# Output projections with the tokens in the partitions, and the seams between the layers in a fixed order

## The chip, the cores and the metric

The kernel runs on one core of a Trainium2 chip. The metric is device time in microseconds (us) of one execution. The core's engines are TensorE (PE, with its weight loads as PEld), VectorE (DVE), ScalarE (ACT), GpSimd (POOL) and SyncE (SP), which issues all the transfers here.

## The reference

The model is three layers over 512 tokens of width 1024: gated linear attention (GLA), native sparse attention (NSA) and a hybrid layer (stick-breaking attention, a causal pool, two branches). What the change touches are the joints between them:

```python
for i in range(2):                                   # i = 0: GLA, i = 1: NSA
    h = rms_norm(x, pre_norm[i])
    y = gla_mixer(h, ...) if i == 0 else nsa_mixer(h, ...)   # each ends in  o @ w_out
    x = x + rms_norm(y, post_norm[i])
# the hybrid layer
h = rms_norm(x, norm_gain) * (1 + scale) + shift     # shift, scale, gate from c
...
merged = sigmoid(m_a) * p_a + sigmoid(m_b) * p_b
x = x + gate * (merged @ w_out)
return rms_norm(x, final_gain)
```

## The kernel before, in words

Activations lie feature-major: `x` is [128 features, 8 chunks, 512 tokens]. Every product in near full precision is three matmuls in fp32r: operands are split into a high part (cast on ACT) and the rest (subtraction on DVE), and high x high, high x low and low x high are summed in PSUM. The activations' parts are `hH` and `hL`; a weight unit is 256 columns wide, comes as two halves through two raw buffers (L147), and is split by `load_unit` (ACT L150, DVE L151) into one of two buffers. `ORDER` lists the units, `prefetch` loads one ahead, a `None` in it is stepped over by `go_on`. PSUM is cut into banks by tag: `pj` 2, `sc` 3, `tr` 2, `pv` 1.

The order of instructions on each engine is found by the compiler's list scheduler, except in the slot loop of the stick-breaking stage, which stands in a `manual_schedule` of PE, DVE, ACT and POOL: there the order of the text holds, and weight splits are put in it by steps (`step`, `run_splits`).

The joints are `boundary` (L326): the layer's output product `out` (L240 to L242) makes feature tiles of 128 x 256 tokens; a token's norm is a sum over partitions, so squares are added up (`Squares`, L279 to L283), reduced with a ones-matmul (L289), put through `rsqrt` (some 13 small DVE steps), and spread over the partitions again with a diagonal matmul (`spread`, L299 and L300). `post` scales, adds the old `x` and squares again; `pre` does the second norm. At the first joint `pre` only gives `rc` and `rT`, one over the row norm, which NSA's consumers multiply in later (token projections L747 to L750, the rope tables, L809, L989). Products, `post` and `pre` of the two token halves are interleaved. Behind the first joint come the token projections of NSA (`w_tok`, 280 columns, L249 to L251), then units 4 and 7 at 512 columns (L208 to L210), from which `compress` (first matmul L828) is fed.

Behind the second joint come v of the first two groups (`sb_vs`), then q and k of group 0, then the slot loop `SB_SLOTS`: each slot scores a pair of heads (L1119, then ACT, POOL and DVE up to the POOL product `SW`, L1140), while PE does listed projections in pieces (L217 to L219) and the products of the pair before (transposes L401, products L1169). The last projections, of u, stay in their two `pj` banks and are copied out by `pool_diff` (L1251). The last product (`w_o2`) is again feature-major, with the final norm behind it (L1339 to L1346).

## Time and profile before

| | us |
|---|---|
| median of 3 runs | 1273.79 (1273.69 to 1275.81) |
| the profiled execution | 1269.81 |
| its span on the chip | 1268.1 |
| PE busy in the span | 1200.2 |
| DVE, ACT, POOL busy | 832.8, 610.1, 312.2 |
| mean granted clock of TensorE | 0.978 of 2.4 GHz |

A row of the view in order of time gives start, length, engine, line, operation and tiles; what stands in brackets is the idle time of that engine before it and what ended it. Matmuls overlap, so the distance from one start to the next is the price, not the length. A granted clock of 1.00 is 2.4 GHz, 0.50 is 1.2 GHz.

### The profile page before, as it was taken

Reading aid. Unit: us, or ns where it says so; the run is one execution under the profiler, and the core shown is the slowest. Engines: PE = TensorE matmul, PEld = TensorE weight load, DVE = VectorE, ACT = ScalarE, POOL = GpSimd, SP = SyncE. Lnnn points to the kernel's source line nnn. Section 1 sums busy time; section 2 is a strip of 40 time slices with the busy share of each in tenths; the row PEclk is TensorE's granted clock in tenths of the full one; section 3 lists DMA queues with packets and bytes.
Section 4 is the critical chain, followed back from the end, with each engine's and each line's share of the span. In section 5 each row is a group of like instructions: output and inputs, shape, how many; then the busy total and the mean of one; then the engine's idle time right before and its main releaser. Section 6 shows DMA issues by size and latency. Waiting matters only on the chain.

```text
span 1268.1 us, 18606 instructions
## 1 busy us (share of the span) xinstructions
PE 1200.2 (95%) x6800; PEld 1014.3 (80%) x6800; DVE 832.8 (66%) x1608; ACT 610.1 (48%) x1274; POOL 312.2 (25%) x432
## 2 busy tenths in 40 slices
PE   6999999889999999999999989999989999999996
PEld 6788778877866777777988968889868888888896
DVE  7678787675569888877578576777765453233554
ACT  6552136533437667669556566575543232212330
POOL 2123122221002433334121264555523400000000
PEclk9999999979999999999999989999989999999998
DMA  6254624325241011110343111111222222333332
GB/s 203 68 179 154 231 93 143 105 93 185 109 125 50 26 51 35 50 34 34 117 134 117 51 50 67 68 67 57 77 83 86 97 79 88 99 100 100 100 117 83
DMA packets 46362, 120.65 MB, mean 95 GB/s; under 512 B 5296, under 2 KB 19760, under 8 KB 45760
## 3 DMA queue, kind: packets, MB, share of 16 engines
q1 hardware_dynamic: 46272, 119.48, 28.7%
q8 instruction: 53, 0.87, 0.3%
q14 instruction: 37, 0.30, 0.1%
HBM read 109.50 MB, written 6.29 MB: 91 GB/s over the span
## 4 chain that ended last, share of the span: by engine, by line
PE 70%; DVE 10%; issue 7%; ACT 6%; DMA 4%; POOL 2%; SPq 0%; DVEq 0%; POOLq 0%; ACTq 0%
PE ps_pj L208 10%; PE ps_pj L209 10%; PE ps_pj L210 10%; PE ps_tr L401 3%; PE ps_pv L971 3%; PE ps_sc L209 2%; PE ps_sc L208 2%; PE ps_sc L210 2%; DVE w_lo L151 2%; PE ps_pj L217 2%; PE ps_pj L219 2%; PE ps_pj L218 2%; DMA wada<-in_w_ada_dram 2%; ACT w_hi L150 1%; PE ps_sc L828 1%
## 5 line engine op out<-in xcount | busy, mean ns | idle before, releaser
L208 PE MATMUL ps_pj<-hH,w_hi 128*128 128x512 f32 (+1 forms) x752 | 281.5, 375 | 9.4 <-DVE u L1251 5.9
L210 PE MATMUL ps_pj<-hH,w_lo 128*128 128x512 f32 (+1 forms) x752 | 280.8, 374 | 0.5 <-DVE w_lo L151 0.5
L209 PE MATMUL ps_pj<-hL,w_hi 128*128 128x512 f32 (+1 forms) x752 | 279.6, 372 | 0.0
L151 DVE TENSOR_TENSOR w_lo<-w_raw,w_hi 128x1024 fp32r<-128x1024 f32 (+1 forms) x154 | 190.4, 1248 | 101.0 <-ACT w_hi L150 101.0
L150 ACT CAST w_hi<-w_raw 128x1024 fp32r<-128x1024 f32 (+1 forms) x154 | 158.9, 1050 | 180.1 <-PE ps_pj L209 66.0
L208 PEld LDWEIGHTS ps_pj<-hH,w_hi 128*128 128x128 f32 x752 | 143.0, 190 | 35.1 <-DVE u L1251 6.0
L210 PEld LDWEIGHTS ps_pj<-hH,w_lo 128*128 128x128 f32 x752 | 143.3, 191 | 23.7 <-DVE w_lo L151 1.0
L209 PEld LDWEIGHTS ps_pj<-hL,w_hi 128*128 128x128 f32 x752 | 143.1, 190 | 23.3 <-issue 0.2
L959 POOL TENSOR_SCALAR PB<-PB,sm 128x128 f32<-128x128 f32 (+3 forms) x128 | 76.9, 621 | 183.6 <-DVE sm L955 183.6
L405 ACT CAST PTh<-ps_tr 128x512 fp32r<-128x512 f32 (+3 forms) x160 | 74.8, 480 | 65.8 <-PE ps_tr L401 61.8
L406 DVE TENSOR_TENSOR PTl<-ps_tr,PTh 128x512 fp32r<-128x512 f32 (+3 forms) x160 | 85.8, 550 | 27.0 <-ACT PTh L405 26.0
L952 ACT ACTIVATE PB<-ps_sc,nmx 128x128 f32<-128x128 f32 (+3 forms) x128 | 66.7, 533 | 16.8 <-PE ps_tr L401 5.5
L217 PE MATMUL ps_pj<-hH,w_hi 128*128 128x512 f32 x176 | 72.0, 409 | 0.0
L219 PE MATMUL ps_pj<-hH,w_lo 128*128 128x512 f32 x176 | 70.2, 399 | 0.0
L218 PE MATMUL ps_pj<-hL,w_hi 128*128 128x512 f32 x176 | 69.9, 397 | 0.0
L1136 DVE TENSOR_TENSOR_SCAN SF<-be,zero 128x128 f32<-128x128 f32 (+3 forms) x64 | 57.2, 915 | 11.6 <-POOL be L1129 11.3
L1140 POOL TENSOR_TENSOR SW<-sg,SF 128x512 f32<-128x512 f32 (+2 forms) x48 | 64.6, 1351 | 0.0
L401 PE MATMUL ps_tr<-ident,PB 128*128 128x128 f32 x320 | 50.9, 273 | 0.0
L249 PE MATMUL ps_pj<-w_hi,hH 128*128 128x256 f32 (+2 forms) x128 | 40.1, 316 | 9.8 <-ACT w_hi L485 8.3
L283 DVE TENSOR_TENSOR acc<-acc,sq 128x256 f32<-128x256 f32 x68 | 31.6, 465 | 24.4 <-ACT sq L282 17.5
L971 PE MATMUL ps_pv<-PTh,vv 128*128 128x512 f32 (+3 forms) x128 | 44.6, 355 | 0.7
L949 DVE TENSOR_REDUCE nmx<-ps_sc 128x1 f32<-128x384 f32 (+1 forms) x64 | 38.9, 617 | 9.6 <-PE ps_sc L948 9.1
(337 smaller groups left out, 2832.5 us busy)
## 6 DMA issues: line engine op xcount, KB each, us to landing
w_raw<-in_w_in_dram SPq DMA_DIRECT2D x64, 512.0 KB, 3.3
wada<-in_w_ada_dram SPq DMA_DIRECT2D x24, 512.0 KB, 3.7
w_raw<-in_w_nsa_dram SPq DMA_DIRECT2D x24, 512.0 KB, 3.9
w_raw<-in_w_gla_dram SPq DMA_DIRECT2D x22, 512.0 KB, 4.3
w_raw<-in_w_gla_out_dram SPq DMA_DIRECT2D x8, 512.0 KB, 3.6
w_raw<-in_w_nsa_out_dram SPq DMA_DIRECT2D x8, 512.0 KB, 3.3
w_raw<-in_w_bb_dram SPq DMA_DIRECT2D x8, 512.0 KB, 3.3
w_raw<-in_w_ba_dram SPq DMA_DIRECT2D x8, 512.0 KB, 3.6
```

The costliest lines, as they stand in the source:

```text
L150: S.copy(hi[:, :, s], raw)
L151: V.tensor_sub(lo[:, :, s], raw, f32(hi[:, :, s]))
L208: TE.matmul(p[:m, :tn], wh[:, k, s], aH[:, k, ts], start=(k == 0), stop=False)
L209: TE.matmul(p[:m, :tn], wh[:, k, s], aL[:, k, ts], start=False, stop=False)
L210: TE.matmul(p[:m, :tn], wl[:, k, s], aH[:, k, ts], start=False, stop=(k == KC - 1))
L217: TE.matmul(p, wh[:, k, s], aH[:, k], start=(k == 0), stop=False)
L218: TE.matmul(p, wh[:, k, s], aL[:, k], start=False, stop=False)
L219: TE.matmul(p, wl[:, k, s], aH[:, k], start=False, stop=(k == KC - 1))
L401: TE.transpose(pt[:, o:o + P], ws[e][:, OFF[qb] + kb * P:OFF[qb] + (kb + 1) * P], ident)
L406: V.tensor_sub(pl[:, :m], pt[:, :m], f32(ph[:, :m]))
L959: G.tensor_scalar(pbs[b][:, o], pbs[b][:, o], sm[:, qb, b:b + 1], 0.0, op0=ALU.mult, op1=ALU.add)
L971: TE.matmul(pv[:, kb * P:], vv[:, kb, b, g].rearrange("p e d -> p (e d)"), p_, start=first, stop=last and p_ is pair[1])
```

## The change

- The three output products (`w_gla_out`, `w_nsa_out`, `w_o2`) have the tokens in the partitions: eight blocks of 128 tokens x 512 features, two units of 256 columns each (`out_products`). The residual `x` is kept and reloaded token-major (`xR`, `x1d`, `x2d`, `xt`). A row's norm is then a sum along the free axis: `square_sum` on ACT with its accumulator, `rms` on DVE, gains as rows spread by a transfer (`row_of`). At the two joints the normed rows are transposed back on PE, eight transposes for a block of tokens, scaled on ACT, and split into `hH` and `hL`. `rc` and `rT` are gone from NSA.
- Each joint stands in a `manual_schedule` (`in_order`) from its first split to behind the first projections of the next layer; the second one goes on through the slot loop. Norm steps are generators in `chains`, moved on by `tick`; `need` moves them on where a projection wants their columns.
- Units 4 and 7 are projected by token halves, before the token projections of the second half; the rope of unit 4 stands in front of those.
- In `SB_SLOTS` the projection k(1, 0) moves from slot 1 to slot 0. u is copied out of PSUM in the slot loop.

```diff
@@ SB_SLOTS
-    ((0, 0), (("q", 1, 0), ("q", 1, 1))),
-    ((0, 1), (("k", 1, 0), ("k", 1, 1), ("za", 0, 0))),
+    ((0, 0), (("q", 1, 0), ("q", 1, 1), ("k", 1, 0))),
+    ((0, 1), (("k", 1, 1), ("za", 0, 0))),
@@ load_unit
+                splits.append((step + (late or lag) + j, hi, split))
+    def tick():
+        nonlocal step
+        step += 1
+        for ch in chains[:]:
+            while ch[0] <= step:
+                d = next(ch[1], None)
+                if d is None:
+                    chains.remove(ch)
+                    break
+                ch[0] = step + d
+        run_splits()
+    @contextmanager
+    def in_order():
+        nonlocal splits
+        E = mybir.EngineType
+        with tc.manual_schedule(engines={E.PE, E.DVE, E.Activation, E.Pool}):
+            splits = []
+            yield
+            while chains:
+                tick()
+            while splits:
+                splits.pop(0)[2]()
+        splits = None
@@ proj_toks (feats_pieces ticks every second k)
         for k in range(KC):
+            if need:
+                if k % max(1, 4 // len(jobs)) == 0:
+                    tick()
+                    ensure(*(u for u, _, _, _ in jobs))
+                need(jobs[0][1] * P, k)
...
+    def rms(ss):
+        v = npl.tile([P, 1], F32, tag="rsv1", name="rsv", bufs=2)
+        V.scalar_tensor_tensor(v, ss[:, 0:1], EPS, ss[:, 1:2], op0=ALU.add, op1=ALU.add)
+        return rsqrt(v, 1)
+    def square_sum(src, ss, n):
+        scr = npl.tile([P, 512], F32, tag="scr", name="scr", bufs=1)
+        S.activation(scr, src, AF.Square, scale=1.0 / 32, accum_out=ss[:, n:n + 1])
+    def out_products(us, each, freed=lambda: None):
+        for c in range(KC):
+            split_h(c, slice(0, 256), x[:, c, 0:256])
+        def second():
+            for c in range(KC):
+                split_h(c, slice(256, 512), x[:, c, 256:512])
+                yield c % 2
+        chains.append([step + 1, second()])
+        for b, n in ((0, 0), (1, 0), (2, 0), (0, 1), (1, 1), (3, 0), (2, 1), (3, 1)):
+            p = psum("sc" if b % 2 else "pj")
+            for i in range(2):
+                proj_toks([(us[2 * n + i], b, p[:, 256 * i:256 * i + 256], 256)], hH, hL, lambda t0, k: None)
+            each(b, n, p)
+            if (b, n) == (3, 0):
+                freed()
+    def boundary(wsrc, gain, xsrc, keep, scale, shift, then):
+        norms_, chunks = {}, [0] * NB
+        def norm(b, ss, xo):
+            y = rms(ss)
+            ss2 = npl.tile([P, 2], F32, tag="ss2", name="ss2", bufs=2)
+            for n in range(2):
+                xn_ = xt[:, b, half(n)]
+                V.scalar_tensor_tensor(xn_, xn_, y, grow[:, half(n)], op0=ALU.mult, op1=ALU.mult)
+                V.tensor_add(xn_, xn_, xo[n])
+                square_sum(xn_, ss2, n)
+            nc.sync.dma_start(keep[:, b], xt[:, b])
+            yield 4
+            y = rms(ss2)
+            xs = [npl.tile([P, 512], F32, tag="xs", name="xs", bufs=2) for n in range(2)]
+            for n in range(2):
+                S.activation(xs[n], xt[:, b, half(n)], AF.Copy, scale=y)
+            yield 4
+            ts = slice(b * P, b * P + P)
+            for n in range(2):
+                pt = psum("tr")
+                for i in range(4):
+                    TE.transpose(pt[:, i * P:(i + 1) * P], xs[n][:, i * P:(i + 1) * P], ident)
...
+                S.copy(hH[:, cs, ts], tmp)
+                V.tensor_sub(hL[:, cs, ts], tmp, f32(hH[:, cs, ts]))
+                chunks[b] += 4
+                yield 1
...
+        def each(b, n, p):
+            if n == 0:
+                SS[b] = npl.tile([P, 2], F32, tag="ss", name="ss", bufs=4)
+            S.copy(xt[:, b, half(n)], p)
+            square_sum(p, SS[b], n)
+            if n:
+                norms_[b] = [step + 2, norm(b, SS[b], [reload(xsrc, b, n_) for n_ in range(2)])]
+                chains.append(norms_[b])
+                if b == 2:
+                    nus.append(unit(*then[0]))
+        with tc.tile_pool(name="wout", bufs=2) as pool:
+            us = [unit(wsrc, u) for u in range(2)]
+            us += [load_unit(wsrc, u, pool=pool, late=4 * u - 3) for u in (2, 3)]
+            grow = row_of(gain)
+            out_products(us, each, go_on)
+            nus.append(unit(*then[1]))
@@ behind the first joint
+            ucs = [load_unit(w_nsa, u, pool=fp, late=5 + 4 * i) for i, u in enumerate((4, 7))]
...
+            toks((0, 1), ("pj", "pj", "sc", "sc"))
+            cks(0)
+            cks(256)
+        r1, r2 = rope(*PCK[0])
+        toks((2, 3), ("tr", "tr", "sc", "pv"))
@@ before the second joint
+    gated = dp.tile([KC, P], F32, name="gated")
+    nc.sync.dma_start(gated.rearrange("c p -> p c"), mod[:, 16:24])
@@ sb_proj
-                UP.append(p)
+                UP.append(u_first.tile([P, T], F32, name="u%d" % j))
+                V.tensor_copy(UP[j], p)
@@ the last product
+        x2 = pool.tile([P, NB, D], F32, name="x2", bufs=1)
+        nc.sync.dma_start(x2, x2d)
+        gate, fgain = row_of(gated.rearrange("c p -> (c p)")), row_of(fgain_r, "fgain")
+        def last(b):
+            y = rms(SS[b])
+            for n in range(2):
+                xn_ = xt[:, b, half(n)]
+                V.scalar_tensor_tensor(xn_, xn_, y, fgain[:, half(n)], op0=ALU.mult, op1=ALU.mult)
+                nc.sync.dma_start(out[:, b, half(n)], xn_)
+            yield 0
+        def each(b, n, p):
...
+            V.tensor_mul(xn_, p, gate[:, half(n)])
+            V.tensor_add(xn_, xn_, x2[:, b, half(n)])
+            square_sum(xn_, SS[b], n)
+            if n:
+                chains.append([step + 1, last(b)])
+        out_products(us, each)
```

## Rows read from the trace of the kernel before

**Rows 1.** The page, busy time, share of the span and instructions of each engine.
```profile
PE 1200.2 (95%) x6800; PEld 1014.3 (80%) x6800; DVE 832.8 (66%) x1608; ACT 610.1 (48%) x1274; POOL 312.2 (25%) x432
```
**Rows 2.** Waits of PE, whole run: us in total, times, longest.
```profile
PE ps_tr L289 <- DVE acc L283: 9.8, 4, 2.8
...
PE ps_tr L300 <- DVE rsd L299: 7.8, 5, 3.5
PE ps_pj L208 <- DVE u L1251: 5.9, 1, 5.9
PE ps_tr L401 <- POOL SW L1140: 5.0, 1, 5.0
```
**Rows 3.** PE in order of time: prices of 256 and 280 columns and of transposes.
```profile
238.46 0.28 PE L240 MATMUL ps_pj<-hH,w_hi 128*128 128x256 f32 x1
...
244.22 0.28 PE L240 MATMUL ps_sc<-hH,w_hi 128*128 128x256 f32 x1
...
263.74 0.28 PE L249 MATMUL ps_sc<-w_hi,hH 128*128 128x280 f32 x1
...
266.44 0.29 PE L249 MATMUL ps_sc<-w_hi,hH 128*128 128x280 f32 x1
...
603.54 1.06 PE L401 MATMUL ps_tr<-ident,PB 128*128 128x128 f32 x8
```
**Rows 4.** PE at the first seam's ends; then windows (PE, PEld, DVE, ACT, POOL, clock, DMA).
```profile
199.47 0.36 PE L240 MATMUL ps_pj<-hH,w_hi 128*128 128x256 f32 x1
...
317.68 2.58 PE L828 MATMUL ps_sc<-csp,cw 128*128 128x124 f32 x21 [1.31 <-issue]
...
275.00:280.00 5.00, 1.49 (x8) 1.37 (x7) 4.59 (x22) 1.56 (x5) 2.46 (x4) 0.50 0.65 214
```
**Rows 5.** DVE in order of time: subtractions of weights at two entries.
```profile
205.93 2.45 DVE L151 TENSOR_TENSOR w_lo<-w_raw,w_hi 128x1024 fp32r<-128x1024 f32 x2
...
1210.71 1.22 DVE L151 TENSOR_TENSOR w_lo<-w_raw,w_hi 128x1024 fp32r<-128x1024 f32 x1
```
**Rows 6.** PE in order of time, second seam: first product, last chunk, slot loop.
```profile
608.26 0.28 PE L240 MATMUL ps_pj<-hH,w_hi 128*128 128x256 f32 x1
...
618.20 0.51 PE L240 MATMUL ps_pj<-hH,w_hi 128*128 128x256 f32 x2 [0.50 <-ACT hH L304]
...
718.32 0.45 PE L217 MATMUL ps_pj<-hH,w_hi 128*128 128x512 f32 x1
```
**Rows 7.** POOL in order of time, first slot; then a window behind it.
```profile
735.14 3.03 POOL L1140 TENSOR_TENSOR SW<-sg,SF 128x512 f32<-128x512 f32 x2
...
740.00:760.00 20.00, 20.00 (x98) 16.72 (x96) 15.00 (x21) 12.77 (x24) 12.72 (x16) 0.95 0.16 53
```
**Rows 8.** Windows: the stretch behind the wait for u.
```profile
940.00:960.00 20.00, 20.00 (x81) 15.99 (x80) 14.65 (x27) 6.36 (x10) 7.49 (x10) 0.91 0.20 70
```
**Rows 9.** All engines in order of time: the last product and the tail.
```profile
1207.37 0.28 PE L208 MATMUL ps_pj<-hH,w_hi 128*128 128x256 f32 x1
...
1255.21 0.48 DVE L1339 SCALAR_TENSOR_TENSOR x<-ps_pj,mod,xr 128x256 f32<-128x256 f32 x1 [1.42 <-PE ps_pj L210]
...
1257.42 0.16 DVE L291 TENSOR_SCALAR rsv<-ps_tr 128x2 f32<-128x2 f32 x1 [0.76 <-PE ps_tr L289]
...
1259.59 0.16 DVE L266 SCALAR_TENSOR_TENSOR rsy<-rst,rsy 128x2 f32<-128x2 f32 x1
...
1261.45 3.22 DVE L1344 SCALAR_TENSOR_TENSOR x<-x,vec,ps_tr 128x256 f32<-128x256 f32 x8 [1.18 <-PE ps_tr L300]
```
**Rows 10.** Groups by line and shape: count, busy us, mean ns, idle before.
```profile
L405 ACT CAST PTh<-ps_tr 128x512 fp32r<-128x512 f32 x64 | 37.3, 586 | 24.0 <-PE ps_tr L401 23.4
...
L406 DVE TENSOR_TENSOR PTl<-ps_tr,PTh 128x512 fp32r<-128x512 f32 x64 | 43.2, 681 | 12.9 <-ACT PTh L405 12.7
```
**Rows 11.** DMA issues by line: count, KB each, median us to landing.
```profile
w_raw<-in_w_nsa_out_dram SPq DMA_DIRECT2D x8, 512.0 KB, 3.3
...
pe<-in_pe_k_dram SPq DMA_DIRECT2D x1, 8.0 KB, 8.3
```

More of the change, by code (lines that the diff above doesn't have):

```diff
@@ L155, in load_unit, with run_splits, ensure @@
             else:
-                splits.append((step + 2 + j, split))
+                splits.append((step + (late or lag) + j, hi, split))
         return hi, lo
-    def run_splits(all_=False):
-        while splits and (all_ or splits[0][0] <= step):
-            splits.pop(0)[1]()
-            if not all_:
-                return
+    def run_splits():
+        if splits and splits[0][0] <= step:
+            splits.pop(0)[2]()
+    def ensure(*units):
+        while splits and any(s_[1] is u_[0] for s_ in splits for u_ in units):
+            splits.pop(0)[2]()
+    def tick():
[19 more added lines that the diff above has]
+            while splits:
+                splits.pop(0)[2]()
+        splits = None
     ORDER = [(w_gla, u) for u in (8, 0, 2, 5, 6, 1, 3, 9, 10)]
-    ORDER += [(w_gla_out, 0), (w_gla_out, 1), None, (w_tok, 0), (w_tok, 1)]
-    ORDER += [(w_nsa, u) for u in (4, 7, 5, 6)]
+    ORDER += [(w_gla_out, 0), (w_gla_out, 1), None, (w_tok, 0), (w_tok, 1), None]
+    ORDER += [(w_nsa, u) for u in (5, 6)]
     ORDER += [(w_nsa, st_[1] + (8 if st_[0] == "z" else 0)) for st_ in NSA_STEPS if st_[0] in ("q", "z")]
@@ L299, in spread @@
             V.tensor_scalar(d, ident, y[:, b:b + 1], None, op0=ALU.mult)
-            TE.matmul(r[:, b * P:(b + 1) * P], ones, d, start=True, stop=True)
+            ds.append(d)
+        return ds
+    def spread(ds):
+        r = psum("tr")
+        for b in range(2):
+            TE.matmul(r[:, b * P:(b + 1) * P], ones, ds[b], start=True, stop=True)
         return r[:, :256]
@@ new lines, in row_scales, with half @@
+        S.copy(rT[:, t0:t0 + 256], spread(diagonals(y)))
+    xt = x.rearrange("p c t -> p (c t)").rearrange("p (b d) -> p b d", b=NB)
+    def half(n):
+        return slice(n * 512, n * 512 + 512)
+    def rms(ss):
[5 more added lines that the diff above has]
+        S.activation(scr, src, AF.Square, scale=1.0 / 32, accum_out=ss[:, n:n + 1])
@@ L706, in tile_kernel @@
         dump("gla_og", gz[:])
-    x1d = dp.tile([P, KC, T], F32, name="x1d")
-    rest = boundary(w_gla_out, "post0", xT, "pre1", keep=x1d)
+    x1d = dp.tile([P, NB, D], F32, name="x1d")
+    norms.close()
+    open_norms()
+    lag = 5
+    prefetch(2)
+    first = ExitStack()
+    first.enter_context(in_order())
+    o = VEC["pre1"][0]
+    uts, need = boundary(w_gla_out, post_r0, xR, x1d, vec[:, o:o + 8], None, ((w_tok, 0), (w_tok, 1)))
     dump("x1", x[:])
@@ L1201, in tile_kernel @@
         pvs = sb_pv()
-        E = mybir.EngineType
-        splits = []
-        with tc.manual_schedule(engines={E.PE, E.DVE, E.Activation, E.Pool}):
-            for n, (pair, prs) in enumerate(SB_SLOTS):
-                scores = sb_w(*pair) if pair else iter(())
-                projs = (None for pr_ in prs for _ in sb_proj(*pr_))
-                if n == 1:
-                    next(pvs)
-                for i in range(8):
-                    step += 1
-                    run_splits()
-                    if n and (n, i) != (1, 0):
-                        next(pvs, None)
-                    next(scores, None)
-                    for _ in range(4 * len(prs) * (i + 1) // 8 - 4 * len(prs) * i // 8):
-                        next(projs)
-                    if n:
-                        next(pvs, None)
-                for _ in projs:
-                    pass
-            for _ in pvs:
-                pass
-            run_splits(True)
-        splits = None
+        lag = 2
+        for n, (pair, prs) in enumerate(SB_SLOTS):
+            scores = sb_w(*pair) if pair else iter(())
+            projs = (None for pr_ in prs for _ in sb_proj(*pr_))
+            if n == 1:
+                next(pvs)
+            for i in range(8):
+                tick()
+                if n and (n, i) != (1, 0):
+                    next(pvs, None)
+                next(scores, None)
+                for _ in range(4 * len(prs) * (i + 1) // 8 - 4 * len(prs) * i // 8):
+                    next(projs)
+                if n:
+                    next(pvs, None)
+            for _ in projs:
+                pass
+        for _ in pvs:
+            pass
+        first.close()
         dump("sb_og", x[:])
@@ L1246, in pool_diff @@
             for j in range(2):
[L1247 to L1248 removed]
+                if ready:
+                    u0 = ready[j]
+                else:
+                    p = psum("pj")
                     proj_feat(uu, j, p, hH, hL)
[L1250 to L1251 removed]
+                    u0 = gp.tile([P, T], F32, tag="zt", name="u0", bufs=4)
+                    V.tensor_copy(u0, p)
                 cur = u0
```

276 lines of the change are left out of this document (120 added, 156 removed).

## The prediction, made before the changed kernel had run

> **What bounds the kernel now.** I read the page first: PE is busy in 95% of the span, no other engine in more than 66% [rows 1]. So PE's own work sets the time, and a change that leaves PE's columns alone can only win PE's idle time and the time it runs at half clock. The view of waits, for PE alone over the whole run, says who PE waits for [rows 2]: the sum of squares (9.8 us) and the spread of the row norm (7.8), both in the seams; the copy of u behind the stick-breaking stage (5.9, once); the product SW at the start of that stage (5.0, once). PE's idle time is 1268.1 - 1200.2 = 67.9 us in all; the four kinds above are 28.5 of it. Last I read PE in order of time in the seams, as the diff rewrites those. The sum is made against the profiled execution (1269.8 us, span 1268.1); the median of the runs shown is 4.0 higher, so the saving is taken off 1273.8 at the end.
>
> **Prices of PE's work at full clock**, as start-to-start times [rows 3]: 48 matmuls of 256 columns from 238.46 to 244.22, 0.120 each; 21 of 280 columns from 263.74 to 266.44, 0.129 each; eight transposes in 1.06, of which the last is some 0.27 long, so 0.11 each or less.
>
> **First seam (GLA output product to the compressed units).** Before, it runs from PE's first product at 199.47 to the first matmul of the compression at 317.68, 118.2 us [rows 4]. After, PE must do in the same stretch: 384 products of 256 columns, 46.1; 192 token projections of 280 columns, 24.7; units 4 and 7 in halves, 2 units x 2 x 2 halves x 24 = 192 of 256, 23.0 (96 of 512 columns before); and, new, 4 blocks x 8 transposes back, 32 x 0.11 = 3.5. The last 8 transposes of the GLA gate also lie in it, 0.8. Sum 98.1. What goes: the ones-matmuls over the squares, the spreads and the waits for them (one of the worst stretches, 275 to 280, has PE busy 1.49 of 5 us at clock 0.50 [rows 4]). What comes:
> - The entry. The auto order filled it with products of four tiles; now PE takes block (0,0) alone, and its second half needs both halves of unit 1's low part. DVE finished those at about 207.1 (first of the two at 205.93, 1.2 each) [rows 5]; PE would be there at about 203.3 to 204.2. I take 3.0, bounds 1.0 (if DVE takes that subtraction ahead of the second-half splits) and 3.8.
> - The row norm. By ticks of 12 matmuls (1.44 us) a block's transposes are emitted 8 ticks, 11.5 us, behind its norm. The chain needs: ten small DVE steps, 2.2 (a like row of them runs from 1257.42 to 1259.59 [rows 9]); four 512-wide DVE steps, 2.7 (0.68 each [rows 10]); the last square on ACT with its accumulator, about 0.8 (0.59 for a 512-wide ACT step [rows 10], and the read-out); 2.2 again; two scalings 1.2. That is 9.1 of 11.5. Blocks 0 and 1 are ready before the token projection asks, blocks 2 and 3 while it and the compressed units run. Cost 0, bounds 0 and 2 a block.
> - The rope of unit 4, its eight copies and the four adds now hide behind 96 token matmuls, 12.4 us; before, they hid behind unit 7's second product and the compression still waited 1.31 [rows 4]. 0.5, bounds 0 and 3.
>
> 98.1 + 3.0 + 0.5 = 101.6, so 16.6 us less; bounds 11 and 19.
>
> **Second seam (NSA output to the first scores).** Before: products from 608.26, the last NSA tile ready at 618.20, the first pieces of the slot loop at 718.32 [rows 6]. By 618.20 PE had already run 55 of 384 products. After, in order, it can run only 21 before chunk 7 is wanted. Left then: 363 x 0.120 = 43.6; tokens for v, 192 x 0.120 = 23.0; q and k by halves, 23.0; 32 transposes, 3.5. Sum 93.1, against 100.1 from 618.20: 7.0 less. Against it: PE idles some 4 us at the entry and starts again at half clock, about 1.0 (as behind the 5.0 us wait below); and the v, q, k tiles of the second half come out two at a time and in order, each bank waiting for an ACT and a DVE step, about 1.3. In its favour: ACT no longer has a weight cast in front of chunk 7's split, about 0.7. Gain 5.4; bounds 0 and 8.
>
> **The slot loop's start.** PE waits 5.0 for the POOL product SW, the two last of which run from 735.14 [rows 7], then runs at a mean granted clock of 0.95 over 20 us (a part at 1.2 GHz, the rest at 2.4), another 1.0. One more projection is moved into slot 0: 24 matmuls of 512 columns, not over 48 x 0.120 = 5.8 us of PE, which covers the wait. Slot 1 loses the same work, so part of the wait may come back there, and ACT and DVE have one more k tile in slot 0. Gain 4.5 of 6.0; bounds 0 and 6.
>
> **u.** The wait of 5.9 [rows 2] and 20 us at 0.91 behind it, 1.8 [rows 8], exist because two banks hold u until the stage's memory is freed. The copies (two of 0.68) now stand in the loop, and no wait for the next unit's splits is listed there. Gain 7.5; bounds 5.9 and 7.7.
>
> **Last product and tail.** Before, PE ends at 1255.2 and the span 12.9 later: one step and square, sum, ones-matmul, the rsqrt chain, spread, eight scalings, stores [rows 9]. After: 384 x 0.120 = 46.1 from 1207.4 [rows 9], plus the entry: unit 1's low part ends at 1211.9 (1210.71 + 1.22 [rows 5]), wanted at 1210.4, so 1.6. PE ends at 1255.1. Then multiply and add 1.4, square and accumulator 0.8, crossings 0.3, rsqrt 2.2, two scalings 1.3, stores 3.4 (last scaling before to the end: 1261.45 + 3.22 to 1268.1): 9.4. Gain 3.6; bounds 1 and 6. The reload of 2 MB of x2 in one transfer waits for the branch stage's memory; 0.5 MB takes 3.3 to land [rows 11], so 2 MB takes up to 13, and the first add wants it after 6. DVE then waits, PE does not, as four tiles lie between: 0, and 3 if the split of unit 3 slips behind it.
>
> **What costs nothing.** The rT multiplications of the z units (eight, DVE) go, but PE has no gap to win there. The write of gated has 1024 pieces of 4 bytes. The nearest row is an 8 KB load of 128 rows of 64 bytes, 8.3 us to landing [rows 11], queued with others. Its source is ready since the GLA stage and nothing reads gated until the end, so I take 0; the upper end is a rival below. The Trainium skill (DMA: Bandwidth & Descriptors, Rules for kernel authors) speaks against this write: a strided last dimension becomes one descriptor for each element. No row here shows such a write.
>
> **The sum.** 16.6 + 5.4 + 4.5 + 7.5 + 3.6 = 37.6. 1269.8 - 37.6 = 1232.2 for a profiled execution; 1273.8 - 37.6 = **1236** by the median. With all bounds at once the gain is 18 to 47; I give the forecast's own range as 1227 to 1250.
>
> **Rivals.**
> - *The ticks are too short.* ACT and DVE now take splits, evictions and norm steps in one fixed list. The chain leaves 2.4 of 11.5 us a block; a weight split in between takes DVE 1.22 a half [rows 5] and nearly as much on ACT, twice a unit, and six units fall in each seam. If two splits and an eviction fall in each block's chain, PE stands at the transposes for about 3 us, 8 blocks: 24 us. 1260. For it: PE can't pass its transposes. Against: most blocks have slack before their columns are wanted.
> - *Slower: casts that wait for their landing.* In ACT's list a cast stands at a set tick; if its transfer is late, evictions, squares, DVE's steps and PE's transposes all queue behind it. Its issue waits for one of two raw buffers, freed by the split before, and landing takes 3.3 [rows 11]. It decides once a cast waits longer than the 5.8 us that one spare tile of product gives PE. Then each of six units stops PE for 3.3 and 1.0 of half clock, 26 us a seam, 52 in both: 1288. Against: the code leaves 5 ticks (7.2 us) between issue and cast.
> - *The write of gated holds the queues* in front of the second seam. If each of its 1024 pieces takes what a row of the 8 KB load takes, it lasts 8 x 8.3 = 66 us [rows 11]; issued as the seam begins, it lets unit 2, wanted after 17 us, land some 45 late: 1281. Against: it can go out long before.
> - *It doesn't do what it says*: the seams end no sooner because the order is fixed only on four engines and SP's list stays automatic; only u and the slot remain or are lost again: 1262 to 1274.
>
> **How the numbers follow.** Forecast 0.70 (1227 to 1250); better than that 0.03; ticks too short 0.14 (1250 to 1270); no effect 0.05, half of it within 0.2%; casts that wait 0.06; gated 0.02. The range 1226 to 1256 takes in the forecast and the near half of the first rival, about 0.8. A measurement of this kernel tells about 0.2% (2.5 us) from no change: faster 0.89, same 0.03, slower 0.08.
>
> **What would show it.** Right: no PE wait on squares or spreads; the first seam about 102 us from the first product to the compression; the second about 95 from the last NSA chunk; no wait for SW over 2 us; the projection behind u following at once; 9 to 10 us from PE's end to the span's. Wrong: PE waiting at the new transposes for xs, or at a product for w_hi or w_lo in mid-seam; a new wait for SW in slot 1 or 2; a compression that waits for its added tokens; an end of PE's last product later than 48 us after its start.

## The result, and the profile of the changed kernel

The changed kernel takes 1290.05 us (median; 1288.54 to 1292.27), the kernel before, measured beside it, 1274.8. The ratio is 1.0117 (95% interval 1.0093 to 1.0141): 1.2% slower, where 3% faster was forecast. Its profiled execution has a span of 1290.3 us and PE's row of the page reads:

```profile
PE 1199.9 (93%) x6880; PEld 1018.1 (79%) x6880; DVE 808.9 (63%) x1534; ACT 626.7 (49%) x1308; POOL 279.9 (22%) x398
```

PE is busy for as long as before (1200.2, [rows 1]). All of the 22.2 us more is PE's idle time: 90.4 instead of 67.9. (The busy time holds what PE does at the lower clock, on which more below.) Cut at marks that both kernels have (first product of the GLA output projection, first score of the NSA stage, its last product, first piece of the slot loop, the loop's last product, first matmul of the last output projection), the span divides so:

| stretch, us of the profiled execution | before | after | forecast | measured |
|---|---|---|---|---|
| start to the GLA output projection | 199.5 | 202.3 | 0 | +2.8 |
| first seam: to the first NSA score | 177.0 | 188.2 | -16.6 | +11.2 |
| NSA stage: to its last product | 237.9 | 236.0 | 0 | -1.9 |
| second seam: to the slot loop | 103.9 | 124.8 | -5.4 | +20.9 |
| slot loop | 214.6 | 213.6 | -4.5 | -1.0 |
| from there to the last output projection | 274.5 | 268.7 | -7.5 | -5.8 |
| last output projection and tail | 60.7 | 56.8 | -3.6 | -3.9 |

(Before, 28 products of the second seam, 3.4 us, are done in the row above it, so 3.4 of the two measured numbers there cancel. One trace tells such a stretch to about 3 us: e4 below, whose seams are those of the kernel before, has 178.6 for the first seam and 106.7 for the second, against 177.0 and 103.9.) Three of the five terms came out with the right sign, the last two of them at about the right size. Both seams came out the other way, by 27.8 and 22.9 us if the 3.4 is taken off. The whole-run view of waits, for PE alone (line waited for, engine and line that ended the wait; total us, times, longest), has the squares of [rows 2] no more, has 0.5, 0.8 and 0.6 us left of the spreads, SW and u, and has this instead:

```profile
PE ps_pj L287 <- ACT w_hi L149: 16.5, 2, 8.5
PE ps_sc L287 <- ACT w_hi L149: 10.3, 3, 4.0
...
PE ps_pj L289 <- DVE hL L357: 4.3, 3, 2.4
...
PE ps_tr L442 <- ACT xs L436: 2.8, 2, 1.6
...
PE ps_pv L1285 <- DVE ov L1292: 2.2, 1, 2.2
...
PE ps_pj L236 <- DVE zt L1400: 1.3, 1, 1.3
```

PE waits for weight casts (L149), not for the row norm: only 2.8 us are spent at the new transposes (L442). The timeline of PE has the four long waits, one pair in each seam, always at the first product of a unit that follows the output projection: token units 0 and 1, then v units 8 and 9.

```profile
264.54 0.60 PE L287 MATMUL ps_pj<-w_hi,hH 128*128 128x280 f32 x1 [8.03 <-ACT w_hi L149]
...
278.11 0.60 PE L287 MATMUL ps_sc<-w_hi,hH 128*128 128x280 f32 x1 [3.78 <-ACT w_hi L149]
...
686.83 0.58 PE L287 MATMUL ps_pj<-w_hi,hH 128*128 128x256 f32 x1 [8.45 <-ACT w_hi L149]
...
700.51 0.42 PE L287 MATMUL ps_sc<-w_hi,hH 128*128 128x256 f32 x1 [4.01 <-ACT w_hi L149]
```

Why is the cast late? The timeline of SP, which issues the weights, shows the two halves of token unit 0 leaving at 222.84:

```profile
222.84 2.46 SPq L146 DMA_DIRECT2D w_raw<-in_w_tok_dram  x2
...
256.87 0.33 SPq L146 DMA_DIRECT2D w_raw<-in_w_tok_dram  x1
```

These loads take 4.2 us to land (median of the four, in the table of transfers), so they lay there by about 230. ACT's timeline in the stretch where PE stops (start, duration, line; in brackets the idle time before it and who ended it):

```profile
253.30 0.58 ACT L467 COPY x<-ps_pj 128x512 f32<-128x512 f32 x1
...
254.36 1.13 ACT L149 CAST w_hi<-w_raw 128x1120 fp32r<-128x1120 f32 x1
255.37 1.16 ACT L447 ACTIVATE ntmp<-ps_tr,vec 128x128 f32<-128x128 f32 x4
256.56 0.62 ACT L452 CAST hH<-ntmp 128x512 fp32r<-128x512 f32 x1
261.30 0.63 ACT L384 ACTIVATE scr<-x 128x512 f32<-128x512 f32 x1 [4.12 <-DVE x L429]
...
262.75 0.63 ACT L384 ACTIVATE scr<-x 128x512 f32<-128x512 f32 x1 [0.73 <-DVE x L429]
...
263.38 1.11 ACT L149 CAST w_hi<-w_raw 128x1120 fp32r<-128x1120 f32 x1
```

The second cast of token unit 0, for which PE stands from 256.51 to 264.54, is next in ACT's list behind the two squares of block 2's norm (L384). ACT does nothing for 4.12 us until DVE has the first half of block 2 ready, squares it, idles 0.73 for the other half, squares that, and only then casts a weight whose transfer had landed by about 230, some 33 us before. (L149 and L150 are the two halves of a weight split, L384 a sum of squares, L428 and L429 the scaling and adding of the first norm, L447 and L452 the eviction of the transposes.) DVE, in the same stretch:

```profile
257.21 0.69 DVE L453 TENSOR_TENSOR hL<-ntmp,hH 128x512 fp32r<-128x512 f32 x1 [0.37 <-ACT hH L452]
257.82 0.15 DVE L379 SCALAR_TENSOR_TENSOR rsv<-ss 128x1 f32<-128x1 f32 x1
...
259.59 0.16 DVE L307 SCALAR_TENSOR_TENSOR rsy<-rst,rsy 128x1 f32<-128x1 f32 x1
259.79 0.75 DVE L428 SCALAR_TENSOR_TENSOR x<-x,rsy,grow 128x512 f32<-128x512 f32 x1
...
261.97 0.69 DVE L429 TENSOR_TENSOR x<-x,xr 128x512 f32<-128x512 f32 x1
...
264.52 1.33 DVE L150 TENSOR_TENSOR w_lo<-w_raw,w_hi 128x1120 fp32r<-128x1120 f32 x1 [1.86 <-ACT w_hi L149]
```

DVE starts block 2's rsqrt at 257.82, late, because it first waited for ACT's hH; then ACT waits for DVE's scaling, and DVE in turn 1.86 for ACT's cast. Neither engine is full (49% and 63% of the run; 11.50 and 13.78 of 20 us in the row of 260 to 280 below). They wait for each other in two fixed lists, and PE waits for both. That ACT keeps to its list whatever is ready behind its head is what the Trainium skill (PSUM — Partial Sum Buffer, Engine vs sequencer instructions) states: ScalarE's and VectorE's queues are strictly first in, first out. This trace agrees, with the 4.12 us ahead of a ready cast.

Behind the waits PE runs slower. Two stretches of the first seam (length, PE busy, ..., granted clock, DMA share, GB/s):

```profile
260.00:280.00 20.00, 10.16 (x51) 9.31 (x52) 13.78 (x35) 11.50 (x24) 0.58 (x1) 0.68 0.34 121
280.00:300.00 20.00, 18.41 (x134) 17.98 (x133) 10.22 (x24) 11.57 (x27) 0.00 (x0) 0.89 0.44 130
```

From 265.90 to 274.33 stand 47 products of 280 columns, 0.179 each instead of the 0.129 of [rows 3]. The first seam up to its last token product took 124.7 us (202.27 to 326.93): 98.1 of work by the prediction's count, 18.5 idle, and 8.0 that are left for slower running. (The mean granted clock of this stretch is 0.92; of the 106.1 us that PE is busy in it, the missing 0.08 are 8.5.)

### The profile page after: what moved, and what is told of

It reads as the page before. It is cut to its first block, busy times and chain, and to the rows that moved or that the text cites. A ratio compares the mean times of both kernels' runs of the same rounds, so it can differ in the third digit from the quotient of the medians.

```text
span 1290.3 us, 18597 instructions
## 1 busy us (share of the span) xinstructions
PE 1199.9 (93%) x6880; PEld 1018.1 (79%) x6880; DVE 808.9 (63%) x1534; ACT 626.7 (49%) x1308; POOL 279.9 (22%) x398
## 4 chain that ended last, share of the span: by engine, by line
PE 57%; DVE 17%; ACT 11%; issue 7%; DMA 4%; POOL 4%; SPq 0%; DVEq 0%; ACTq 0%; POOLq 0%
PE ps_pj L236 6%; PE ps_pj L238 6%; PE ps_pj L237 5%; ACT w_hi L149 3%; DVE w_lo L150 3%; PE ps_tr L494 3%; PE ps_pv L1082 2%; PE ps_sc L238 2%; PE ps_sc L237 2%; PE ps_sc L236 2%; ACT PB L1063 2%; PE ps_pj L245 2%; POOL us L1375 2%; PE ps_pj L247 2%; PE ps_pj L246 2%
## 5 line engine op out<-in xcount | busy, mean ns | idle before, releaser
L150 DVE TENSOR_TENSOR w_lo<-w_raw,w_hi 128x1024 fp32r<-128x1024 f32 (+1 forms) x154 | 189.4, 1242 | 118.8 <-ACT w_hi L149 114.0
L149 ACT CAST w_hi<-w_raw 128x1024 fp32r<-128x1024 f32 (+1 forms) x154 | 159.2, 1050 | 151.3 <-PE ps_sc L237 62.4
L236 PE MATMUL ps_pj<-hH,w_hi 128*128 128x512 f32 x528 | 213.8, 405 | 7.8 <-DVE rtm L843 3.8
L237 PE MATMUL ps_pj<-hL,w_hi 128*128 128x512 f32 x528 | 211.9, 401 | 0.0
L238 PE MATMUL ps_pj<-hH,w_lo 128*128 128x512 f32 x528 | 211.8, 401 | 0.0
L238 PEld LDWEIGHTS ps_pj<-hH,w_lo 128*128 128x128 f32 x528 | 100.0, 189 | 20.9
L287 PE MATMUL ps_sc<-w_hi,hH 128*128 128x256 f32 (+1 forms) x312 | 92.5, 298 | 10.8 <-ACT w_hi L149 10.3
L289 PE MATMUL ps_pj<-w_hi,hL 128*128 128x256 f32 (+2 forms) x304 | 90.3, 298 | 4.3 <-DVE hL L357 4.3
L288 PE MATMUL ps_pj<-w_lo,hH 128*128 128x256 f32 (+2 forms) x304 | 90.7, 298 | 3.0 <-DVE w_lo L150 1.7
L288 PE MATMUL ps_sc<-w_lo,hH 128*128 128x256 f32 (+1 forms) x312 | 91.5, 293 | 1.8 <-DVE w_lo L150 1.8
L289 PE MATMUL ps_sc<-w_hi,hL 128*128 128x256 f32 (+1 forms) x312 | 90.5, 291 | 0.0
L287 PEld LDWEIGHTS ps_pj<-w_hi,hH 128*128 128x128 f32 x304 | 61.4, 202 | 30.0 <-ACT w_hi L149 16.9
L245 PE MATMUL ps_pj<-hH,w_hi 128*128 128x512 f32 x176 | 71.1, 404 | 0.5 <-DVE SQs L1166 0.5
L287 PEld LDWEIGHTS ps_sc<-w_hi,hH 128*128 128x128 f32 x312 | 61.7, 199 | 11.5 <-ACT w_hi L149 10.8
L247 PE MATMUL ps_pj<-hH,w_lo 128*128 128x512 f32 x176 | 69.5, 395 | 0.0
```

The costliest lines, as they stand in the source:

```text
L149: S.copy(hi[:, :, s], raw)
L150: lo_on[j].tensor_sub(lo[:, :, s], raw, f32(hi[:, :, s]))
L236: TE.matmul(p[:m, :tn], wh[:, k, s], aH[:, k, ts], start=(k == 0), stop=False)
L237: TE.matmul(p[:m, :tn], wh[:, k, s], aL[:, k, ts], start=False, stop=False)
L238: TE.matmul(p[:m, :tn], wl[:, k, s], aH[:, k, ts], start=False, stop=(k == KC - 1))
L245: TE.matmul(p, wh[:, k, s], aH[:, k], start=(k == 0), stop=False)
```

## The experiments

The theory after this reading is *head of the line*: a step emitted for ACT together with the DVE steps that it needs blocks ACT for their whole length, and what stands behind it comes late, whatever that is. Its rivals: the casts wait for their transfers (*landing*, a rival of the prediction), and ACT and DVE together have too much to do in the seam (*full engines*). All runs, with the two stretches of the table above (before 177.0 and 103.9, changed 188.2 and 124.8). The kernel before was run again beside each group of runs, so the ratios are what compares across the rows; the changed kernel's is 1.0117 (1.0093 to 1.0141):

| run | median us | ratio to before (95%) | first seam | second seam |
|---|---|---|---|---|
| e1 casts early | 1280.9 | 1.0067 (1.0048 to 1.0086) | 182.4 | 120.7 |
| e2 norms late | 1285.2 | 1.0102 (1.0081 to 1.0122) | 184.2 | 125.3 |
| e3 both | 1284.5 | 1.0098 (1.0076 to 1.0120) | 182.6 | 123.8 |
| e7 splits first | 1278.6 | 1.0029 (1.0014 to 1.0045) | 181.8 | 119.7 |
| e5 five pieces | 1260.0 | 0.9891 (0.9867 to 0.9916) | 175.1 | 110.9 |
| e6 five pieces, casts early | 1258.3 | 0.9880 (0.9858 to 0.9901) | 171.1 | 108.4 |
| e8 five pieces, splits first | 1262.3 | 0.9917 (0.9893 to 0.9940) | 173.3 | 111.3 |
| e9 rsqrt sooner | 1259.2 | 0.9889 (0.9863 to 0.9915) | 171.8 | 110.4 |
| e12 scaling sooner | 1259.3 | 0.9890 (0.9867 to 0.9914) | 171.5 | 110.8 |
| e10 low parts on POOL | 1262.8 | 0.9915 (0.9890 to 0.9941) | 172.0 | 110.5 |
| e11 as e9, slots back | 1261.4 | 0.9902 (0.9878 to 0.9925) | 171.5 | 109.0 |
| e4 before, with u and slot | 1266.1 | 0.9948 (0.9922 to 0.9973) | 178.6 | 106.7 |

### Moving what waits: e1, e2, e3

e1 emits the casts of the two units behind the output product sooner:

```diff
-            ahead.append((o_, load_unit(*o_, n=280 if o_[0] is w_tok else 256)))
+            first_, second_ = ((o_[0] is w_tok and o_[1] == i) or (o_[0] is w_in2 and o_[1] == 8 + i) for i in (0, 1))
+            ahead.append((o_, load_unit(*o_, n=280 if o_[0] is w_tok else 256,
+                                        late=1 if first_ else 2 if second_ else None)))
```

> The changed kernel with one thing moved: in both seams the weight casts of the two units behind the output product (the token units, and the two v units of the second seam) are emitted 1 and 2 ticks after their loads, instead of 5. Three theories of the waits of 8.0 and 3.8 us (first seam) and 8.5 and 4.0 (second) that PE shows for those casts. List: the cast is ready and stands in ACT's list behind the two squares of block 2's norm, which wait for DVE; with both casts of the first unit now ahead of these squares, the waits of 8.0 and 8.5 fall below 3 each, those of 3.8 and 4.0 shrink by half or stay, and the time is about 1267 (1262 to 1275). Landing: the casts wait for their transfers or for a raw buffer; an earlier place in the list changes nothing, the waits stay and the time is 1287 to 1292. Full engines: ACT and DVE have more to do in the seam than PE; the wait moves to the transposes or to later units, and the time stays within 5 us of 1290.

e2 starts the norm chains of blocks 2 and 3 later:

```diff
-                norms_[b] = [step + 2, norm(b, SS[b], [reload(xsrc, b, n_) for n_ in range(2)])]
+                norms_[b] = [step + (2, 2, 8, 6)[b], norm(b, SS[b], [reload(xsrc, b, n_) for n_ in range(2)])]
```

> The changed kernel with one other thing moved: the norm chains of blocks 2 and 3 start 8 and 6 ticks after their last product instead of 2, so that the casts of the two units behind the output product come ahead of their squares. List: no cast of the two units is left behind a step that waits for DVE's norm of block 2 or 3; the waits of 8.0 and 8.5 us fall to about 3, those of 3.8 and 4.0 to 1 or less; about 1260 (1254 to 1272). Landing: the waits stay, 1287 to 1292. Full engines: the columns of blocks 2 and 3 come too late now and PE waits for them at the second half of the units in halves, as long as it waited before: 1283 to 1292.

e3 has both edits.

> Both moves in one kernel. List: about 1256 (1250 to 1266), the first seam from 124.7 us (first product to the last token product) to 105 to 110, the second from 124.8 to 104 to 110. Landing: 1287 to 1292. Full engines: 1280 to 1292.

*Landing* is out: the four waits went in e1 and e3 and fell to 1.7 and 2.2 for the first units in e2, with the same transfers. But by the ratios the gains over the changed kernel are only some 6 us in e1 and about 2 in e2 and e3, and the intervals of these two overlap that of the changed kernel. None of the three came near the time of *head of the line* (List in the expectations; 1267, 1260 and 1256); e2 and e3 lie in the range of *full engines*. New waits stand elsewhere: 4.9 us for block 1's hH and 4.9 for unit 4's cast in e1, 6.1 for unit 4's cast in e2 and e3. ACT's timeline in e3, ahead of that last wait:

```profile
267.72 1.06 ACT L149 CAST w_hi<-w_raw 128x1024 fp32r<-128x1024 f32 x1
273.50 0.63 ACT L386 ACTIVATE scr<-x 128x512 f32<-128x512 f32 x1 [4.72 <-DVE x L431]
...
274.89 0.63 ACT L386 ACTIVATE scr<-x 128x512 f32<-128x512 f32 x1 [0.67 <-DVE x L431]
...
275.52 1.03 ACT L149 CAST w_hi<-w_raw 128x1024 fp32r<-128x1024 f32 x1
```

The pattern is the same, one block and one unit later: unit 4's second cast behind block 3's squares, ACT idle for 4.72 and 0.67. By these runs *full engines* stood as well as *head of the line*, since both foresee that a wait moves on when its victim is moved.

### Moving what blocks: e7, e5, e6, e8

e7 puts the splits ahead of the norm steps of the same tick; e5 leaves the splits and emits the chain in five pieces, ACT's steps when DVE should be through:

```diff
         step += 1
+        run_splits()
...
-        run_splits()
```

> The changed kernel with two calls in the tick swapped: a weight split that is due is emitted ahead of the norm steps of the same tick, not behind them. The second casts of both units fall on the ticks on which the norms of blocks 2 and 3 start, and unit 4's second on the tick of block 2's scaling. Head of the line: the waits of 8.0 and 8.5 fall to 3 or less, those of 3.8 and 4.0 too, about 1264 (1256 to 1276). Full engines: 1280 to 1292.

```diff
                 V.tensor_add(xn_, xn_, xo[n])
-                square_sum(xn_, ss2, n)
             nc.sync.dma_start(keep[:, b], xt[:, b])
             yield 4
+            for n in range(2):
+                square_sum(xt[:, b, half(n)], ss2, n)
+            yield 1
             y = rms(ss2)
+            yield 2
...
                 S.activation(xs[n], xt[:, b, half(n)], AF.Copy, scale=y)
-            yield 4
+            yield 2
```

> The changed kernel with the norm chain emitted in five pieces instead of three: DVE's rsqrt, scaling and adding first, ACT's two squares 4 ticks later, DVE's second rsqrt 1 tick after them, ACT's scaling 2 ticks after that, the transposes 2 after that. No instruction more or less; a block's transposes come 1 tick later. In the runs before, moving the casts or the norms alone took away the waits of 8 us and others came up: unit 4's second cast then stood behind block 3's two squares, for which ACT waited 4.7 for DVE. Head of the line: whatever stands behind an ACT step that was emitted together with the DVE steps it needs waits for all of them (5 us); with the ACT steps emitted when DVE is done, PE's waits for casts fall to 3 or less in both seams and the time is about 1258 (1250 to 1270). Full engines: nothing was taken from ACT or DVE, so the waits only move on and the time is 1278 to 1292. Late low parts: DVE's own list has the rsqrt and the scaling ahead of the second low part of the first token unit; if that is what binds, PE waits 3 to 5 there in each seam and the time is 1268 to 1278.

e6 is e5 with e1's edit, e8 is e5 with e7's.

> The five pieces, and with them the casts of the two units behind the output product 1 and 2 ticks after their loads. Head of the line: about 1253 (1247 to 1266), as DVE's low parts of the first unit now also come ahead of block 2's norm. Full engines: 1278 to 1292.

> The five pieces and the splits first. Head of the line: about 1253 (1246 to 1266). Full engines: 1278 to 1292.

e7 once more moved the victim; its 1278.6 lies between the ranges of the two theories (1256 to 1276 and 1280 to 1292). Both casts now run in one go, and behind the squares stands the eviction of block 1's transposes (L447, L452), for which PE waits 4.2 and 4.7 instead:

```profile
250.97 2.15 ACT L149 CAST w_hi<-w_raw 128x1120 fp32r<-128x1120 f32 x2
...
258.94 0.63 ACT L384 ACTIVATE scr<-x 128x512 f32<-128x512 f32 x1 [4.12 <-DVE x L429]
...
261.02 1.12 ACT L447 ACTIVATE ntmp<-ps_tr,vec 128x128 f32<-128x128 f32 x4
262.18 0.62 ACT L452 CAST hH<-ntmp 128x512 fp32r<-128x512 f32 x1
```

e5 has the same instructions on every engine as the changed kernel and moves no cast, and takes 30 us less (1260.0 for 1290.05; 29 by the ratios to the kernel before). In its ACT timeline the two squares follow the cast at once, with no idle time ahead of either; ACT's next wait, 3.69, is for a transfer:

```profile
256.07 1.12 ACT L149 CAST w_hi<-w_raw 128x1120 fp32r<-128x1120 f32 x1
257.09 0.64 ACT L384 ACTIVATE scr<-x 128x512 f32<-128x512 f32 x1
...
257.84 0.63 ACT L384 ACTIVATE scr<-x 128x512 f32<-128x512 f32 x1
...
262.26 1.13 ACT L149 CAST w_hi<-w_raw 128x1120 fp32r<-128x1120 f32 x1 [3.69 <-DMA w_raw<-in_w_tok_dram]
```

That settles it between *head of the line* and *full engines*: nothing was taken from any engine. The waits of the third case of its expectation came true beside the time of the first. PE's waits in e5:

```profile
PE ps_pj L288 <- DVE w_lo L150: 9.6, 2, 5.0
...
PE ps_tr L445 <- ACT xs L439: 4.4, 6, 1.6
```

The 5.0 and 4.6 are the low part of the first token and v unit, which stands on DVE behind block 2's scaling. With the casts early as well (e6) these go, and the seams are 4.0 and 2.5 us shorter in the traces. The intervals of the two ratios overlap; the medians lie 1.7 us apart, and e6's four times are all below e5's four, so a small gain is likely and not certain. e6 is 1.2% (1.0 to 1.4) faster than the kernel before and, by the two ratios, 2.3% faster than the changed one. e8 gains nothing over e5 (1262.3 for 1260.0, with overlapping intervals).

### What is left: e9, e12, e10

In e6 PE still waits 9.8 us for xs, in eight places. e9 starts the chain one tick sooner and emits the second rsqrt with the squares:

```diff
-            yield 1
             y = rms(ss2)
             yield 2
...
-            yield 2
+            yield 3
...
-                norms_[b] = [step + 2, norm(
+                norms_[b] = [step + 1, norm(
```

> As the run with five pieces and early casts, but the chain starts one tick sooner, the second rsqrt is emitted on the tick of the squares (so ahead of the next block's first DVE steps on DVE), and the transposes 3 ticks behind ACT's scaling. In that run PE still waited for ACT's scaling (xs) 2.3, 0.4 and 1.2 us in the first seam and 2.9, 1.0 and 1.6 in the second, because one block's second rsqrt stood on DVE behind the next block's scaling. If order is all that is left, these go, the seams come from 108 to about 104 each and the time is 1250 (1246 to 1256). If DVE has no more room, waits for hL or w_lo take their place: 1256 to 1262.

e12 then takes ACT's scaling one tick sooner, with `yield 1` and `yield 4` for e9's 2 and 3.

> As the run with the sooner rsqrt, but ACT's scaling (xs) one tick sooner, the transposes where they were. There PE still waits 2.7 and 3.3 us at block 1's transposes, once in each seam: the rsqrt was ready 3.4 us before ACT came to the scaling, as a cast and an eviction of block 0 stood ahead of it. Behind these waits PE runs at a granted clock of 0.79, and of 0.50 and 0.83, for 5 and 10 us. If this is one more step in the wrong place of ACT's list, the waits fall below 1, the clock stays at 1.00 and the time is about 1251 (1247 to 1255): each wait costs about its length again by the clock. If the clock falls whatever PE waits for, or ACT has no more room, 1256 to 1261.

e10 is e9 with some low parts on POOL:

```diff
-                lo_on[j].tensor_sub(lo[:, :, s], raw, f32(hi[:, :, s]))
+                (G if late and j else lo_on[j]).tensor_sub(lo[:, :, s], raw, f32(hi[:, :, s]))
```

> The same, and of the units whose casts have a set tick of their own, the low part of the second half is taken by POOL instead of DVE (1.49 us for 544 columns where the run begins, so an estimated 2.8 for 1024, against 1.23 on DVE). If DVE's list is what still holds PE: 2 to 5 less than the run before it in this list. If not: the same within 2, or up to 5 more where PE waits for POOL.

None of them gained, and all three times lie in the second range of their expectations. e9 has one wait for xs left in each seam (2.71 and 3.27, at block 1's transposes); e12 removed these, and a wait of 3.07 came up 7 us later in the first seam and one of 2.93 in the second, for the low part of block 1's first columns. First e9's, then e12's row:

```profile
248.91 1.11 PE L446 MATMUL ps_tr<-ident,xs 128*128 128x128 f32 x4 [2.71 <-ACT xs L440]
```

```profile
249.93 0.66 PE L446 MATMUL ps_tr<-ident,xs 128*128 128x128 f32 x4 [0.59 <-ACT ntmp L451]
...
257.15 0.60 PE L291 MATMUL ps_pj<-w_hi,hL 128*128 128x280 f32 x1 [3.07 <-DVE hL L457]
```

Here the rows fit *full engines*. Stretches of e12 (columns as above: PE, PEld, DVE, ACT and POOL busy, clock):

```profile
250.00:255.00 5.00, 4.08 (x33) 3.84 (x33) 3.91 (x14) 4.97 (x14) 1.31 (x4) 1.00 0.38 123
255.00:260.00 5.00, 2.85 (x12) 2.85 (x13) 4.97 (x7) 4.52 (x11) 2.78 (x3) 0.61 0.62 185
260.00:265.00 5.00, 5.00 (x30) 5.00 (x29) 4.37 (x23) 1.34 (x2) 0.00 (x0) 0.71 0.54 185
...
660.00:665.00 5.00, 2.07 (x16) 1.75 (x16) 4.90 (x7) 4.97 (x11) 2.80 (x6) 1.00 0.44 152
665.00:670.00 5.00, 5.00 (x45) 5.00 (x44) 4.23 (x20) 2.93 (x9) 0.00 (x0) 1.00 0.70 220
```

ACT is busy for 4.97 of 5 us, then DVE: evictions of two blocks, two casts and a scaling all fall between block 1's last product and the tokens that want it. The two orders tried did not mend that. That no order could is not shown, and no run took work from ACT. Taking low parts from DVE to POOL gained nothing: a low part takes it 2.41 us at the median (DVE 1.22), PE waits up to 2.0 for it, the seams stay as they were, and the last output projection and tail grow from 56.3 to 58.4.

### The parts outside the seams: e4 and e11

e4 is the kernel before with the moved projection and the copies of u alone; e11 is e9 with the projection moved back.

```diff
-    ((0, 0), (("q", 1, 0), ("q", 1, 1))),
-    ((0, 1), (("k", 1, 0), ("k", 1, 1), ("za", 0, 0))),
+    ((0, 0), (("q", 1, 0), ("q", 1, 1), ("k", 1, 0))),
+    ((0, 1), (("k", 1, 1), ("za", 0, 0))),
...
-                UP.append(p)
+                UP.append(u_first.tile([P, T], F32, name="u%d" % j))
+                V.tensor_copy(UP[j], p)
```

> The kernel before with only two parts of the change: the projection moved from slot 1 to slot 0, and u copied to a buffer of its own inside the loop. Seams and last product as before. If the two terms of the prediction stand (4.5 and 7.5), the time is 12 less than before, 1263 (1260 to 1266). The trace of the changed kernel has the whole stretch from the slot loop to the last product only 5.5 shorter than before; if the rest was given back inside that stretch (a wait of 2.2 for ov, one of 0.8 for SW, one of 1.3 for zt), it comes out at about 1269 (1266 to 1271).

> As the run with the sooner rsqrt, with the projection put back from slot 0 into slot 1. If the slot term of the prediction (4.5) holds, 4.5 more; by the traces of the changed kernel and of the kernel before with two parts (1.0 and 2.4 for the whole slot loop) 1 to 2.5 more: the wait of 5.0 for SW comes back and the wait of 2.2 for ov in slot 1 goes.

e4 gains 0.5% (0.3 to 0.8), about 6.6 us, not 12. (The stretch that its expectation has 5.5 shorter in the changed kernel is 6.8 shorter by the table, 1.0 and 5.8.) In its trace the slot loop is 2.4 shorter (214.6 to 212.2) and the stretch behind it 5.5 (274.5 to 269.0). In e11 the slot loop is 3.1 longer than in e9 (216.64 for 213.56), and the medians differ by 2.2, with overlapping intervals. The traces of the changed kernel and of the runs built on it with the same slots have 213.5 to 215.0 for the loop, so e11 stands clear of them, and the 1.0 between the kernel before (214.6) and the changed one does not. In e11 the wait for SW is back:

```profile
736.08 0.47 PE L498 MATMUL ps_tr<-ident,SW 128*128 128x128 f32 x1 [6.32 <-POOL SW L1260]
```

Where the projection stands in slot 0, PE waits in slot 1 instead, here in the changed kernel (e9 has 2.16 there, e4 2.14):

```profile
790.85 0.50 PE L1285 MATMUL ps_pv<-PTh,SV 128*128 128x512 f32 x1 [2.20 <-DVE ov L1292]
```

## Why the prediction was wrong, step by step

**The row norm in the first seam, "cost 0, bounds 0 and 2 a block".** This is the step that failed. It added up one block's chain, 9.1 us, and held it against the 11.5 until the block's own transposes. That sum was sound where nothing stood in the way: block 0's chain took 9.0 us (231.80 to 240.81), block 2's 15.0 (257.82 to 272.85), and the transposes waited only 1.2 us in the first seam and 1.6 in the second. What it left out is who stands *behind* the chain's steps on ACT and DVE. Each joint of the chain (rsqrt and scaling on DVE, then the squares on ACT) was emitted on one tick, so ACT stood still for up to 4.1 us with casts behind it. The diff shows this: `run_splits()` comes last in the tick, and the second casts fall on the ticks on which the norms of blocks 2 and 3 start. Every chain should have been read twice, once for when its end is wanted, and once for what queues behind each link. e5 measures the omission at 29 to 30 us; in the traces 13.1 of it is in the first seam and 13.9 in the second, whose sum has no term for the row norm at all. Of the signs of being wrong that the prediction lists, this one came: PE waiting at a product for `w_hi` in mid-seam.

**The rivals.** *Ticks too short* named the cause in kind, ACT and DVE in one fixed list, but put the waits at the transposes (3 us a block, 24 in all; measured 2.8) and allowed nothing for the clock, so its 1260 was 30 short. *Casts that wait for their landing* was within 2 us of the time, and named the place and the head-of-line blocking, but the wrong trigger, so that its time came out by luck (six stops of 4.3 us a seam, where the trace has two long waits and the slower running behind them): in each seam of the changed kernel ACT waited for a weight transfer once, 1.09 and 1.02 us, in the middle of the output product, and the cast for which PE stood 8 us had had its data for some 26 when PE came to it. Its argument against itself, the 5 ticks between issue and cast, was beside the point. *The write of gated* made no engine wait. Its row in the table of transfers (KB, us to landing) and the one late transfer of the tail:

```profile
gated<-mod SPq DMA_DIRECT2D x1, 4.0 KB, 10.1
```

```profile
1244.22 0.69 DVE L1467 TENSOR_TENSOR x<-x,x 128x512 f32<-128x512 f32 x1 [2.47 <-DMA x<-x2d]
```

1024 pieces of 4 bytes took 10.1 us to land, against the 66 of the rival's price, and went out at 172.1, ahead of both seams. What the rival says of the queues is seen all the same. The two loads of `w_gla_out` issued right behind it took 12.3 and 10.0 us to land, where those of the kernel before, which has no such write, took 3.4 and 3.5 (view of the tile `w_raw`, changed kernel from 172 to 190, then the kernel before from 169 to 190):

```profile
DMA to landing us min/median/max: 10.0/11.1/12.3
```

```profile
DMA to landing us min/median/max: 3.4/3.4/3.5
```

The other traces with the write have 8.9 to 11.8 there, e4, which has none, 3.4 and 3.5. It cost no time because the later of the two landed at 186.8 and its unit's first cast came at 190.28, 3.5 later: the write stood in a place with room to spare, which the prediction did not work out. The rule of the Trainium skill that the prediction weighed (DMA: Bandwidth & Descriptors, Rules for kernel authors) calls for another layout; in these runs nothing waited that another layout would have helped. *It doesn't do what it says* fell too: of the waits that the change was to remove, none is left over 1 us.

**The entry.** 2.41 us in the first seam, against 3.0 (1.0 to 3.8), and 1.35 in the last product, against 1.6. The sizes are right, the wait is not quite the one that was priced. PE stops within the products of unit 0, not for the low part of unit 1, but for an `hL` of the activations that stands on DVE behind both subtractions of unit 1 (the second of them 206.05 to 207.27, the `hL` to 207.60, PE goes on at 207.66).

**The rope of unit 4**, 0.5 (0 to 3): the compression began at 334.50, 7.6 behind the last token product; 4.4 of that PE filled with the next unit (19 products of 0.23). About 3, the upper bound. Its chain is the same in e6 (318.99, 7.6 behind), so this is no effect of the late casts.

**The second seam, 5.4 (0 to 8).** Besides the failed step, the term itself was too high. With the casts and norms in order (e6) the seam still takes 108.4, against 103.9 and the 3.4 done ahead: 1.1 more than before, not 5.4 less (to the 3 us or so that one trace tells). Work of 95.6 (384 + 192 + 192 products of 0.120, 32 transposes) leaves 12.8; 8.5 of it is PE's idle time in that trace, mostly for xs. The first seam, up to its last token product, takes 108.3 in e6, where 101.6 was forecast up to the compression: 7.2 idle instead of 3.5, and 2.9 slower running. So these orders did not reach the forecast's seams; 22 us of the 54 by which it missed remain in the best run (1258.3 against 1236).

**The slot loop, 4.5 (0 to 6).** The wait for SW fell from 5.0 to 0.8 as said, and "part of the wait may come back" in slot 1 as ov: net 1.0 in the changed kernel, 3.1 between e9 and e11. The place was right; the size was too high, and the changed kernel's 1.0 can't be told from none.

**u, 7.5 (5.9 to 7.7).** 5.8, just under the lower bound. The wait of 5.9 is gone and the clock is 1.00 behind it, where [rows 8] had 0.91. The prediction saw no wait behind it; there are two, 0.55 for a copy of the next u (L1369) and 1.28 for zt, in e4 as well (0.54 and 1.17).

**Last product and tail, 3.6 (1 to 6).** 3.9: the product took 47.9 (forecast 47.7), the tail 8.9 (9.4). x2 landed 8.9 after its issue and DVE waited 2.5 for it, PE did not: as said.

**The first stretch, 0.** Its 2.8 is scatter: up to the first product the kernels are nearly the same, and the 14 profiled executions, before and e4 among them, reach it between 198.0 and 203.2. A single trace can't tell less than 5 us there.

## What to carry to other kernels

When an order is written out by hand, an instruction belongs in an engine's list at the place where its inputs are ready, not where the chain is described: the same instructions in five pieces instead of three made 29 us by the ratios, where moving their victims made 2 to 11. When a wait moves on after its victim was moved, look at what ACT or DVE stood idle for just ahead of the victim, and move that. A price for a chain in a fixed list needs two checks, its end against its consumer, and each link against what queues behind it.

## What the runs showed of the hardware

How PE's clock answers a wait of some 3 us is not a fixed price. In e9 the stretches behind the waits of 2.71 and 3.27 read:

```profile
250.00:255.00 5.00, 5.00 (x37) 5.00 (x36) 4.06 (x14) 4.94 (x14) 0.00 (x0) 0.79 0.17 66
...
655.00:660.00 5.00, 4.12 (x20) 4.12 (x21) 2.85 (x12) 4.97 (x12) 0.00 (x0) 0.50 0.33 109
660.00:665.00 5.00, 5.00 (x37) 5.00 (x37) 4.93 (x8) 4.58 (x10) 0.98 (x3) 0.83 0.42 159
```

0.50 is the level of 1.2 GHz. By the share of the clock that was missing, the second wait cost PE 2.9 us more (half of 4.12, and 0.17 of 5.00), the first 1.1 in the stretch shown, e12's 3.07 2.6 (0.39 of 2.85, 0.29 of 5.00), and e12's 2.93, which ended at 663.56, nothing in the rows of 660 to 665 and 665 to 670 shown with it. The prediction took 1.0 for each, from one case. What decides between these is open: no run varied the length of a wait alone.
